# Latent attention: rows of the first two pairs of query tiles loaded ahead, in front of the loads of w_out

## The chip, the cores and the metric

The kernel runs on one core of one Trainium2 chip. The metric is the device time of one execution in microseconds. The engines are TensorE (PE in the rows; PEld is its weight load), VectorE (DVE), ScalarE (ACT), GpSimd (POOL) and SyncE (SP), which here does nothing but issue all transfers between the device memory and the core's buffers.

## What is computed

Two layers. Each one normalises the rows of x (1024 tokens of 1024 numbers), projects them, runs three kinds of heads side by side, projects the joined heads back (w_out) and adds them to x, and then runs a feed-forward block (w_up, w_down). The change is in the second kind of heads, the latent attention, of which this is the reference:

```python
def _mla(cq, ckv, kr, cos, sin, q_norm_g, w_uq, kv_norm_g, w_ukv):
    b, s, _ = cq.shape
    q = (_rmsnorm(cq, q_norm_g) @ w_uq).reshape(b, s, MLA_HEADS, MLA_NOPE + MLA_ROPE)
    qn = q[..., :MLA_NOPE]
    qr = _apply_rope(q[..., MLA_NOPE:], cos[:, :, None, :], sin[:, :, None, :])
    kv = (_rmsnorm(ckv, kv_norm_g) @ w_ukv).reshape(b, s, MLA_HEADS, MLA_NOPE + MLA_V)
    kn, v = kv[..., :MLA_NOPE], kv[..., MLA_NOPE:]
    ...
    def block(args):
        start, qnb, qrb = args
        sc = (jnp.einsum('bqhd,bkhd->bhqk', qnb, kn)
              + jnp.einsum('bqhr,bkr->bhqk', qrb, kr)).astype(jnp.float32) * scale
        p = _masked_softmax(sc, _chunk_mask(start, s))
        return jnp.einsum('bhqk,bkhe->bqhe', p.astype(v.dtype), v)
```

cq has 256 columns and ckv 128, so a tile of 128 tokens has low-rank rows of 128 x 384 numbers. There are 8 such tiles (t = 0 to 7), worked on in four pairs (i = 0 to 3). The mask is causal by chunks of 64 tokens, so pair i needs the keys and values of tiles up to 2i + 1.

## The kernel before

Numbers are 32-bit floats, and each large product is made of three matmuls on numbers split into a high and a low part: L191 to L193 in `mm3`. A split takes ScalarE (L230, the high part) and VectorE (L231, the rest).

**The latent attention.** The in-projection has written the low-rank rows to `d_c` in device memory. `lora(l, st)` loads the weights and gives three functions. `first(t)` loads tile t of `d_c` (L1041, 192 KB), scales it on VectorE (L1042, L1043), and transposes it on TensorE (L1046); `second(t, ...)` multiplies it with w_uq and w_ukv (L1056, L1058); `third` transposes the result (L1085) and splits it (L1089, L1090). In `mla`, `ahead(n, i)` calls them for pair i in four steps, n = 0 to 3. Pair 0 is prepared before the mark `"hidden"`, and pair i + 1 while the scores (L191 to L193, softmax L896 and L897), the product with the values (L922, L909, L938) and the sums of pair i are made.

**What runs beside it.** `mixer` interleaves the instruction streams by `weave`, which always takes the stream that has used the least of a weighted budget. Up to the mark `"hidden"`, the stream of `mla` runs beside the first kind of heads and the end of the in-projection. Then `mla` up to pair 0's heads runs beside the state-space heads (L1230 to L1279, in stream `ip`) and `load_wout`, which loads w_out in 8 pieces of 512 KB (L1288) and splits each on ScalarE (L1292 or L1295) and VectorE (L1296) or GpSimd (L1293). After that, the out-projection (transposes L656, products L191 to L193) runs beside pairs 1 to 3. Before the feed-forward block's first products, each tile of x is normalised (L639), transposed (L212), and its sums and splits are made (L644, L217, L231); its weights w_up come by L270, six narrow loads of 512 KB (128x8x128) first and then wide ones of 1 MB (128x8x256), whose sums are made on GpSimd (L284 to L287) and split. Products are stored to `d_r` by L248. This block is called mlp_up below.

**What sets the order.** All transfers are issued by SyncE, one behind the other: where one waits for its buffer, those behind it wait too. The compiler's scheduler settles each engine's order from the order of the program and from what each instruction waits for. Buffers of one large area (arena_f) are handed out by `Arena`: `get` takes a free place, the one that was given back longest ago, and `put` gives it back. A new holder waits for the old holder's last reader, and so every `get` that is moved or held longer changes the places, and the waits, of later ones, in the whole program.

Of the kernel before, what the change touches and what calls it, by code (L numbers as in the profile page):

```python
# [17 lines left out]
P = 128  # L18
# [12 lines left out]
WOW = 16  # L31
GROUPS = [2] + [4] * 6 + [2, 4]
LEAD = 6
C_Q, C_K, C_V, C_CQ, C_CKV, C_KR, C_Z, C_XBC, C_DT = 0, 256, 512, 768, 1024, 1152, 1184, 1696, 2464

SLOT = 2048
# [70 lines left out]
class Net:  # L107
# [125 lines left out]
    def mlp_up(self, l, hT, bg, late):  # L233
# [27 lines left out]
        N = FF // (2 * P)  # L261
        todo = [(i, True, False) for i in range(LEAD)] + [(i, i >= LEAD, True) for i in range(N)]
        staged = []
# [32 lines left out]
        stage()  # L296
        parts = self.chain(*(forms() for _ in range(LEAD + N)))
        queue = [next(parts) for _ in range(3)]
# [40 lines left out]

        for i in range(LEAD):  # L340
            next(late, None)
# [672 lines left out]
    def lora(self, l, st):  # L1014

        nc, F, I = self.nc, self.F, self.i
        p = st["p"]
        wuq, wukv = F.get(2, 384, top=True), F.get(512, top=True)
# [10 lines left out]
        kr = F.get(8, 32, top=True)  # L1029
# [6 lines left out]
        nc.vector.tensor_add(kr, kr, tmp)  # L1036
        F.put(tmp, k0)

        def first(t):
            cn = F.get(384)  # L1040
            nc.sync.dma_start(cn, self.d_c[l][t * P:t * P + P, 0:384])  # L1041
            nc.vector.tensor_scalar(cn[:, 0:256], cn[:, 0:256], rq[:, t:t + 1], None, op0=ALU.mult)  # L1042
            nc.vector.tensor_scalar(cn[:, 256:384], cn[:, 256:384], rkv[:, t:t + 1], None, op0=ALU.mult)  # L1043
            ps = self.bank("t")[:, 0:384]
            for k in range(3):
                nc.tensor.transpose(ps[:, k * P:k * P + P], cn[:, k * P:k * P + P], self.ident)  # L1046
            F.put(cn)
            cT = F.get(384)
            nc.scalar.copy(cT, ps)
            return cT  # L1050
# [38 lines left out]
                nc.scalar.copy(dst[0:96, :, 0], pv)  # L1089
                nc.vector.tensor_sub(dst[0:96, :, 1], pv, f32(dst[0:96, :, 0]))  # L1090

        return first, second, third, lambda: F.put(kr, wuq, wukv)

    def mla(self, l, st, cc):

        nc, F = self.nc, self.F
        first, second, third, done = self.lora(l, st)
        a, b = {}, {}

        def scores(h, i, pt):  # L1100
            QT, KT = st["QT"][i % 2][:, h], st["KT"][:, h]
            ll, rl = self.sm(2, "ml_l"), self.sm(2, "ml_rl")
            for tt in range(2):
                n = P * (2 * i + tt + 1)
                tok = slice(tt * P, tt * P + P)
                S = self.bank2()
                for c0 in range(0, n, 512):
                    c1 = min(n, c0 + 512)
                    self.mm3(S[:, c0:c1], QT[0:96, 0, tok], QT[0:96, 1, tok],
                             KT[0:96, 0, c0:c1], KT[0:96, 1, c0:c1], True, c1 < n)  # L1110
                nc.tensor.matmul(S[:, n - 64:n], self.chunk[0:96, 0:P], self.chunk[0:96, P:192], start=False, stop=True)  # L1111
                p = F.get(n)
                self.softmax(S, n, p, self.sm(1, "nm"), ll[:, tt:tt + 1])
                pt.append(p)
                yield
            nc.vector.reciprocal(rl, ll)
            pt.append(rl)

        def values(h, i, pt):
            rl = pt.pop()  # L1120
            yield from self.p_times_v(pt[0], pt[1], i, st["vml"][:, :, h], rl, cc[i][:, :, 256 + h * 64:320 + h * 64])
            F.put(*pt)

        def ahead(n, i):
            t = 2 * i
            if n == 0:
                a[t] = first(t)
            elif n == 1:
                a[t + 1] = first(t + 1)
                b[t] = second(t, a.pop(t))  # L1130
            elif n == 2:
                b[t + 1] = second(t + 1, a.pop(t + 1))

        for n in range(3):
            ahead(n, 0)
            yield 2.0
        yield "hidden"
        held, last = iter(()), None
        for i in range(4):
            for t in (2 * i, 2 * i + 1):  # L1140
                third(t, b.pop(t))
                yield 2.0
                next(held, None)
            cc[i] = F.get(2, D, top=True)
            rows = self.d_cc[l][i * 256:i * 256 + 256].rearrange("(t p) e -> p t e", p=P)
            nc.sync.dma_start(cc[i][:, :, 0:256], rows[:, :, 0:256])
            nc.sync.dma_start(cc[i][:, :, 512:1024], rows[:, :, 512:1024])
            for h in range(4):
                pt = []
                for _ in scores(h, i, pt):  # L1150
                    yield 2.0 + 2 * i
                    next(held, None)
                for _ in held:
                    yield 1.0
                if last is not None:
                    yield last
                    last = None
                held = values(h, i, pt)
                if i < 3:
                    ahead(h, i + 1)  # L1160
            last = i
        done()
        for _ in held:
            yield 1.0
        yield last
# [431 lines left out]
```

## Time and profile before

| what | us |
|---|---|
| median of 3 runs | 2828.76 (2823.73 to 2833.22) |
| profiled execution | 2827.39 |
| its span in the trace | 2825.7 |
| TensorE busy in it | 2642.5 (94%) |
| VectorE, ScalarE, GpSimd busy | 1755.9, 1111.0, 587.5 |

TensorE is busy for nearly all of the span, so a gain can come from two things alone: stretches in which TensorE has nothing to do, and stretches in which it runs at the lower of its two clock levels. The mean granted clock of the execution is 0.952 of full speed.

### The profile page before, as it was taken

To read this page: it belongs to the slowest core of one execution; us is meant where nothing else is said; L and a number is where in the kernel's file an instruction comes from. 1 tells how busy PE (TensorE), PEld (TensorE's weight loads), DVE (VectorE), ACT (ScalarE), POOL (GpSimd) and SP (SyncE) were. 2 spreads that over 40 slices of the span, in tenths; PEclk is the share of its full clock that TensorE was granted. 3 is DMA by queue.
4 is the path that set the end of the run, shared out by engine and by line. 5 is a ranking of instruction groups with operands and counts; after the bars stand their busy time and mean duration, and the time that the engine had idled before them with its cause. 6 is when DMAs were issued, how large, how long until landed. Compare 5 with 4: busy or idle time off the path is not lost.

```text
span 2825.7 us, 34756 instructions
## 1 busy us (share of the span) xinstructions
PE 2642.5 (94%) x12530; PEld 2066.1 (73%) x12530; DVE 1755.9 (62%) x3223; ACT 1111.0 (39%) x2145; POOL 587.5 (21%) x517
## 2 busy tenths in 40 slices
PE   5799999899879999999999999988997999999998
PEld 4677776676757777777778777765766888888886
DVE  7767666544867777756585576664459654643435
ACT  5243443544534446121143433354445455621212
POOL 1441233310333220000021113342003522000002
PEclk9899988899989999999999998888998999999999
DMA  6441212322345546534331121132133432541313
GB/s 225 116 137 51 94 50 61 110 73 84 101 150 165 158 148 216 179 122 151 107 119 48 56 91 63 54 101 86 52 105 104 153 116 101 177 149 65 120 47 102
DMA packets 268527, 311.54 MB, mean 110 GB/s; under 512 B 28674, under 2 KB 212164, under 8 KB 268356
## 3 DMA queue, kind: packets, MB, share of 16 engines
q1 hardware_dynamic: 268356, 309.32, 34.0%
q8 instruction: 99, 1.62, 0.2%
q14 instruction: 72, 0.59, 0.1%
HBM read 242.85 MB, written 66.43 MB: 109 GB/s over the span
## 4 chain that ended last, share of the span: by engine, by line
PE 65%; DVE 11%; DMA 7%; issue 2%; ACT 2%; POOL 1%; SPq 0%; DVEq 0%; ACTq 0%; POOLq 0%
PE bank_b L191 9%; PE bank_b L193 9%; PE bank_b L192 9%; PE bank_s L191 8%; PE bank_s L192 8%; PE bank_s L193 8%; PE bank_s L962 3%; DVE split L231 2%; PE bank_a L909 2%; PE bank_t L922 2%; DVE arena_f L570 2%; DMA arena_f<-in_w_ada 1%; DMA d_r<-arena_f 1%; PE bank_s L656 1%; PE bank_a L938 1%
## 5 line engine op out<-in xcount | busy, mean ns | idle before, releaser
L191 PE MATMUL bank_b<-split 128*128 128x512 f32 (+2 forms) x1824 | 728.5, 400 | 51.0 <-ACT split L230 33.1
L192 PE MATMUL bank_b<-split 128*128 128x512 f32 (+2 forms) x1824 | 709.6, 389 | 3.5 <-DVE split L231 3.1
L193 PE MATMUL bank_b<-split 128*128 128x512 f32 (+2 forms) x1824 | 706.5, 389 | 2.9 <-DVE split L231 2.9
L230 ACT CAST split<-arena_f 128x512 fp32r<-128x512 f32 (+1 forms) x424 | 305.8, 747 | 678.3 <-PE bank_s L192 425.8
L191 PE MATMUL bank_s<-split 128*128 128x512 f32 (+2 forms) x1152 | 456.1, 398 | 18.3 <-DVE arena_f L390 6.7
L192 PE MATMUL bank_s<-split 128*128 128x512 f32 (+2 forms) x1152 | 451.2, 392 | 4.4 <-DVE split L231 1.8
L191 PEld LDWEIGHTS bank_b<-split 128*128 128x128 f32 x1824 | 354.1, 194 | 129.5 <-ACT split L230 34.8
L193 PE MATMUL bank_s<-split 128*128 128x512 f32 (+2 forms) x1152 | 448.2, 389 | 0.0
L231 DVE TENSOR_TENSOR split<-arena_f,split 128x512 fp32r<-128x512 f32 (+1 forms) x424 | 381.7, 919 | 92.8 <-ACT split L230 92.0
L193 PEld LDWEIGHTS bank_b<-split 128*128 128x128 f32 x1824 | 352.7, 193 | 71.6 <-DVE split L231 5.0
L192 PEld LDWEIGHTS bank_b<-split 128*128 128x128 f32 x1824 | 354.7, 194 | 68.5 <-issue 4.9
L408 DVE TENSOR_TENSOR arena_f<-arena_f,bank_s 128x1024 f32<-128x1024 f32 x126 | 153.5, 1218 | 230.9 <-PE bank_s L193 230.9
L191 PEld LDWEIGHTS bank_s<-split 128*128 128x128 f32 (+1 forms) x1152 | 218.4, 190 | 73.8 <-DVE arena_f L390 7.4
L192 PEld LDWEIGHTS bank_s<-split 128*128 128x128 f32 (+1 forms) x1152 | 219.5, 191 | 50.4 <-DVE split L231 3.5
L193 PEld LDWEIGHTS bank_s<-split 128*128 128x128 f32 (+1 forms) x1152 | 219.1, 190 | 43.4 <-issue 0.2
L897 ACT ACTIVATE arena_f<-bank_s,nm 128x128 f32<-128x128 f32 (+3 forms) x192 | 141.8, 740 | 191.8 <-DVE nm L896 160.8
L896 DVE TENSOR_REDUCE nm<-bank_s 128x1 f32<-128x128 f32 (+3 forms) x192 | 142.2, 752 | 118.8 <-PE bank_s L1111 64.5
L570 DVE SCALAR_TENSOR_TENSOR arena_f<-arena_f,cond 128x128 f32<-128x128 f32 x448 | 161.7, 387 | 71.4 <-DMA arena_f<-in_b_ada 32.9
L246 ACT ACTIVATE arena_f<-arena_f 128x512 f32<-128x512 f32 x128 | 80.8, 632 | 141.6 <-DVE arena_f L331 69.6
L962 PE MATMUL bank_s<-split 32*128 32x512 f32 (+3 forms) x576 | 124.0, 390 | 12.3 <-ACT arena_f L897 9.1
L925 ACT COPY arena_f<-bank_t 128x512 f32<-128x512 f32 (+1 forms) x160 | 86.8, 542 | 114.1 <-PE bank_t L922 100.9
L696 POOL TENSOR_TENSOR arena_f<-arena_f 128x1024 f32<-128x1024 f32 x14 | 33.6, 2399 | 454.0 <-ACT rstd_y L182 340.0
(281 smaller groups left out, 3207.0 us busy)
## 6 DMA issues: line engine op xcount, KB each, us to landing
arena_f<-in_w_ada SPq DMA_DIRECT2D x80, 512.0 KB
d_r<-arena_f SPq DMA_DIRECT2D x128, 256.0 KB
arena_f<-in_w_up SPq DMA_DIRECT2D x32, 1024.0 KB
arena_f<-in_w_down SPq DMA_DIRECT2D x64, 512.0 KB
arena_f<-d_r SPq DMA_DIRECT2D x64, 512.0 KB
arena_f<-d_x SPq DMA_DIRECT2D x36, 512.0 KB
d_x<-arena_f SPq DMA_DIRECT2D x23, 512.0 KB
arena_f<-in_w_in SPq DMA_DIRECT2D x20, 512.0 KB
```

The source lines that it names most:

```text
L191: mm(out, wh, xh, start=start, stop=False)
L192: mm(out, wh, xl, start=False, stop=False)
L193: mm(out, wl, xh, start=False, stop=stop)
L230: self.nc.scalar.copy(hi, src)
L231: (eng or self.nc.vector).tensor_sub(lo, src, f32(hi))
L246: nc.scalar.activation(t, t, AF.Relu)
L408: nc.vector.tensor_add(y[t], y[t], ps)
L570: nc.vector.scalar_tensor_tensor(acc, in0=w[:, k], scalar=self.cond[:, k:k + 1], in1=acc, op0=ALU.mult, op1=ALU.add)
L896: nc.vector.tensor_reduce(nm, S[:, 0:n], axis=AX.X, op=ALU.max, negate=True)
L897: nc.scalar.activation(p[:, 0:n], S[:, 0:n], AF.Exp, bias=nm, accum_out=ls)
L925: nc.scalar.copy(held, ps[:, 0:w])
L962: nc.tensor.matmul(S[mp][:, c0:c1], Q[rw, a, tok], K[rw, b, c0:c1], start=a == b, stop=a == 1 and c1 < n)
```

## The change

`first(t)` is divided into `load(t)`, which takes the buffer and issues the load, and `first(t, cn)`, which does the rest. `mla` loads tiles 0 and 1 at its start, and tiles 2 and 3 (`EARLY`) when pair 0 is prepared, just ahead of the mark `"hidden"` and so ahead of the loads of w_out in the program. `row(t)` hands out an early buffer or loads the tile as before. In each layer four loads move; no instruction is added or removed, and each early buffer of 384 words is held longer.

```diff
--- before.py
+++ after.py
@@ -31,6 +31,7 @@
 WOW = 16
 GROUPS = [2] + [4] * 6 + [2, 4]
 LEAD = 6
+EARLY = 2, 3
 C_Q, C_K, C_V, C_CQ, C_CKV, C_KR, C_Z, C_XBC, C_DT = 0, 256, 512, 768, 1024, 1152, 1184, 1696, 2464
 
 SLOT = 2048
@@ -1036,9 +1037,12 @@
         nc.vector.tensor_add(kr, kr, tmp)
         F.put(tmp, k0)
 
-        def first(t):
+        def load(t):
             cn = F.get(384)
             nc.sync.dma_start(cn, self.d_c[l][t * P:t * P + P, 0:384])
+            return cn
+
+        def first(t, cn):
             nc.vector.tensor_scalar(cn[:, 0:256], cn[:, 0:256], rq[:, t:t + 1], None, op0=ALU.mult)
             nc.vector.tensor_scalar(cn[:, 256:384], cn[:, 256:384], rkv[:, t:t + 1], None, op0=ALU.mult)
             ps = self.bank("t")[:, 0:384]
@@ -1089,13 +1093,14 @@
                 nc.scalar.copy(dst[0:96, :, 0], pv)
                 nc.vector.tensor_sub(dst[0:96, :, 1], pv, f32(dst[0:96, :, 0]))
 
-        return first, second, third, lambda: F.put(kr, wuq, wukv)
+        return load, first, second, third, lambda: F.put(kr, wuq, wukv)
 
     def mla(self, l, st, cc):
 
         nc, F = self.nc, self.F
-        first, second, third, done = self.lora(l, st)
+        load, first, second, third, done = self.lora(l, st)
         a, b = {}, {}
+        rows = {t: load(t) for t in (0, 1)}
 
         def scores(h, i, pt):
             QT, KT = st["QT"][i % 2][:, h], st["KT"][:, h]
@@ -1121,12 +1126,15 @@
             yield from self.p_times_v(pt[0], pt[1], i, st["vml"][:, :, h], rl, cc[i][:, :, 256 + h * 64:320 + h * 64])
             F.put(*pt)
 
+        def row(t):
+            return rows.pop(t) if t in rows else load(t)
+
         def ahead(n, i):
             t = 2 * i
             if n == 0:
-                a[t] = first(t)
+                a[t] = first(t, row(t))
             elif n == 1:
-                a[t + 1] = first(t + 1)
+                a[t + 1] = first(t + 1, row(t + 1))
                 b[t] = second(t, a.pop(t))
             elif n == 2:
                 b[t + 1] = second(t + 1, a.pop(t + 1))
@@ -1134,6 +1142,8 @@
         for n in range(3):
             ahead(n, 0)
             yield 2.0
+
+        rows.update({t: load(t) for t in EARLY})
         yield "hidden"
         held, last = iter(()), None
         for i in range(4):
@@ -1142,9 +1152,9 @@
                 yield 2.0
                 next(held, None)
             cc[i] = F.get(2, D, top=True)
-            rows = self.d_cc[l][i * 256:i * 256 + 256].rearrange("(t p) e -> p t e", p=P)
-            nc.sync.dma_start(cc[i][:, :, 0:256], rows[:, :, 0:256])
-            nc.sync.dma_start(cc[i][:, :, 512:1024], rows[:, :, 512:1024])
+            src = self.d_cc[l][i * 256:i * 256 + 256].rearrange("(t p) e -> p t e", p=P)
+            nc.sync.dma_start(cc[i][:, :, 0:256], src[:, :, 0:256])
+            nc.sync.dma_start(cc[i][:, :, 512:1024], src[:, :, 512:1024])
             for h in range(4):
                 pt = []
                 for _ in scores(h, i, pt):
```

The scheduler and the arena turn this into other orders on all engines. In what follows, line numbers of the changed kernel are higher: L1042 there is L1041 of before, L1050 is L1046, L1298 is L1288, L1289 is L1279, L1156 and L1157 are L1146 and L1147, L993 is L992; up to L1036 they are higher by one.

SyncE in layer 1, from the load of tile 2 to the next loads of tiles (`d_c`: a tile's rows; `in_w_out`: a piece of w_out; `d_cc`: results of the other heads, stored or loaded). Before:

```order
L1041 DMA arena_f<-d_c_114 128x384
L1279 DMA d_cc_116<-arena_f 128x512
L1288 DMA arena_f<-in_w_out 128x1024 x3
L1147 DMA arena_f<-d_cc_116 128x2x512
L1288 DMA arena_f<-in_w_out 128x1024
L1279 DMA d_cc_116<-arena_f 128x512
L1288 DMA arena_f<-in_w_out 128x1024 x3
L992 DMA d_cc_116<-arena_f 128x8x64
L1146 DMA arena_f<-d_cc_116 128x2x256
L1041 DMA arena_f<-d_c_114 128x384
L1146 DMA arena_f<-d_cc_116 128x2x256
L1147 DMA arena_f<-d_cc_116 128x2x512
```

After the change:

```order
L1289 DMA d_cc_116<-arena_f 128x512
L1042 DMA arena_f<-d_c_114 128x384 x2
L1298 DMA arena_f<-in_w_out 128x1024 x4
L1157 DMA arena_f<-d_cc_116 128x2x512
L1298 DMA arena_f<-in_w_out 128x1024 x3
L1042 DMA arena_f<-d_c_114 128x384
L993 DMA d_cc_116<-arena_f 128x8x64
L1298 DMA arena_f<-in_w_out 128x1024
L1289 DMA d_cc_116<-arena_f 128x512
L1156 DMA arena_f<-d_cc_116 128x2x256
L1042 DMA arena_f<-d_c_114 128x384
L622 DMA arena_f<-d_mod 128x1024
```

Tile 3's load stood behind seven loads of w_out and a store of `d_cc` (L992); now it stands beside tile 2's, ahead of all of them. The last load of w_out stood behind the loads of tiles 3 and 4; now it stands behind tile 4's alone.

TensorE in layer 1, around the transposes of tile 3 (L1046 before, L1050 after; L191 to L193 and L1111 are scores, with L192 to L194 and L1116 after). Before:

```order
L192 MATMUL bank_s<-split 128x128
L193 MATMUL bank_s<-split 128x128
L1111 MATMUL bank_s<-chunk_mask 128x64
L191 MATMUL bank_s<-split 128x256
L192 MATMUL bank_s<-split 128x256
L193 MATMUL bank_s<-split 128x256
L1111 MATMUL bank_s<-chunk_mask 128x64
L1085 MATMUL bank_s<-ident,arena_f 96x128 x8
L1046 MATMUL bank_t<-ident,arena_f 128x128 x3
L922 MATMUL bank_t<-ident,arena_f 128x128 x3
L1056 MATMUL bank_b<-arena_f 128x384 x2
L1058 MATMUL bank_b<-arena_f 128x512
```

After:

```order
L910 MATMUL bank_a<-arena_f 64x256
L910 MATMUL bank_a<-arena_f 64x128
L1050 MATMUL bank_t<-ident,arena_f 128x128 x3
L192 MATMUL bank_s<-split 128x256
L193 MATMUL bank_s<-split 128x256
L194 MATMUL bank_s<-split 128x256
L1116 MATMUL bank_s<-chunk_mask 128x64
L939 MATMUL bank_a<-twice,arena_f 128x64 x2
L923 MATMUL bank_t<-ident,arena_f 128x128 x3
L192 MATMUL bank_s<-split 128x128
L193 MATMUL bank_s<-split 128x128
L194 MATMUL bank_s<-split 128x128
```

The transposes of tile 3 stood behind all scores of pair 0 and behind the eight L1085 of tile 2; now they stand between two groups of scores, ahead of the products L939 and L923.

VectorE in layer 0, at the start of the feed-forward block (L639, L640 after: tile 7 is normalised; L318, L319 after: a product is taken up, the last one from bank_b_6105; L644 and L217, L645 and L218 after: tile 7's transposes are taken up from bank_s_5988; L231, L232 after: splits). Before:

```order
L318 TENSOR_TENSOR arena_f_67<-arena_f_67,bank_b_6069 128x512
L231 TENSOR_TENSOR split_66<-arena_f_67,split_66 128x4x128
L185 TENSOR_SCALAR rstd_t_1_5978<-rstd_y_1_5976,rstd_m_1_5977 128x1
L231 TENSOR_TENSOR split_66<-arena_f_67,split_66 128x512 x2
L186 TENSOR_SCALAR rstd_y_1_5976<-rstd_t_1_5978,rstd_y_1_5976 128x1
L231 TENSOR_TENSOR split_66<-arena_f_67,split_66 128x4x128
L639 SCALAR_TENSOR_TENSOR arena_f_67<-arena_f_67,rstd_y_1_5976 128x1024
L318 TENSOR_TENSOR arena_f_67<-arena_f_67,bank_b_6105 128x512
L644 TENSOR_TENSOR arena_f_67<-bank_s_5988,arena_f_67 128x512
L217 TENSOR_TENSOR arena_f_67<-bank_s_5988,arena_f_67 128x512
L231 TENSOR_TENSOR split_66<-arena_f_67,split_66 128x4x128 x2
```

After, where L640 of tile 7 stands eight rows further up, out of this piece:

```order
L645 TENSOR_TENSOR arena_f_67<-bank_s_5988,arena_f_67 128x512
L218 TENSOR_TENSOR arena_f_67<-bank_s_5988,arena_f_67 128x512
L232 TENSOR_TENSOR split_66<-arena_f_67,split_66 128x4x128
L232 TENSOR_TENSOR split_66<-arena_f_67,split_66 128x512 x2
L232 TENSOR_TENSOR split_66<-arena_f_67,split_66 128x4x128 x2
L319 TENSOR_TENSOR arena_f_67<-arena_f_67,bank_b_6069 128x512
L232 TENSOR_TENSOR split_66<-arena_f_67,split_66 128x4x128
L218 TENSOR_TENSOR arena_f_67<-arena_f_67 128x512 x3
L319 TENSOR_TENSOR arena_f_67<-arena_f_67,bank_b_6105 128x512
L232 TENSOR_TENSOR split_66<-arena_f_67,split_66 128x4x128 x3
L232 TENSOR_TENSOR split_66<-arena_f_67,split_66 128x512 x4
```

Tile 7 was taken up from its transposes behind the last product; now it is taken up ahead of the last two products, and its last splits follow the last product directly.

## Rows read from the trace of the kernel before

**Rows 1.** The page: the span, then from the costliest groups the product matmuls.
```profile
span 2825.7 us, 34756 instructions
...
L191 PE MATMUL bank_b<-split 128*128 128x512 f32 (+2 forms) x1824 | 728.5, 400 | 51.0 <-ACT split L230 33.1
```

**Rows 2.** Waits of TensorE, 1895 to 1925 us (total, times, longest).
```profile
PE bank_t L1046 <- DVE arena_f L1042: 8.7, 1, 8.7
```

**Rows 3.** SyncE, 1840 to 1940 us: start, duration, line, transfer, count.
```profile
1870.84 0.32 SPq L1041 DMA_DIRECT2D arena_f<-d_c  x1
...
1886.12 4.61 SPq L1288 DMA_DIRECT2D arena_f<-in_w_out  x3
...
1898.89 11.01 SPq L1288 DMA_DIRECT2D arena_f<-in_w_out  x3
...
1915.31 0.46 SPq L1041 DMA_DIRECT2D arena_f<-d_c  x1
...
1926.45 0.35 SPq L1288 DMA_DIRECT2D arena_f<-in_w_out  x1
```

**Rows 4.** Chain that ended last, 1880 to 1945 us, in order of time.
```profile
1889.92 3.78 DMA arena_f<-in_w_out
...
1915.31 3.35 DMA arena_f<-d_c
...
1926.45 4.03 DMA arena_f<-in_w_out
...
1937.55 1.77 PE bank_s L656 x8
```

**Rows 5.** Two stretches: width, busy PE, PEld, DVE, ACT, POOL (counts), PEclk, DMA, GB/s.
```profile
1901.70:1925.59 23.89, 11.61 (x36) 7.92 (x36) 13.12 (x42) 8.33 (x20) 10.07 (x8) 0.50 0.39 117
785.80:804.84 19.04, 0.02 (x2) 0.01 (x1) 8.58 (x12) 5.33 (x9) 11.18 (x9) 0.58 0.59 179
```

**Rows 6.** SyncE, 450 to 545 us (layer 0).
```profile
496.07 0.33 SPq L1288 DMA_DIRECT2D arena_f<-in_w_out  x1
...
500.81 0.32 SPq L1041 DMA_DIRECT2D arena_f<-d_c  x1
```

**Rows 7.** Waits of TensorE, 450 to 545 us.
```profile
PE bank_b L1255 <- POOL arena_f L1246: 2.0, 1, 2.0
```

**Rows 8.** ScalarE, 1889 to 1935 us: a split of w_out.
```profile
1930.56 1.15 ACT L1295 ACTIVATE split<-arena_f,cols 128x1024 fp32r<-128x1024 f32 x1 [1.81 <-DMA arena_f<-in_w_out]
```

**Rows 9.** Waits of TensorE, 735 to 812 us (start of mlp_up, layer 0).
```profile
PE bank_b L191 <- ACT split L230: 20.9, 2, 19.0
```

**Rows 10.** Chain that ended last, 765 to 810 us.
```profile
787.08 5.14 DMA d_r<-arena_f
...
792.71 7.79 DMA arena_f<-in_w_up
...
804.16 0.63 ACT split L230
```

**Rows 11.** VectorE, 774 to 812 us: tile 7 and the last product.
```profile
779.50 1.28 DVE L639 SCALAR_TENSOR_TENSOR arena_f<-arena_f,rstd_y 128x1024 f32<-128x1024 f32 x1
785.04 0.69 DVE L318 TENSOR_TENSOR arena_f<-arena_f,bank_b 128x512 f32<-128x512 f32 x1 [4.26 <-PE bank_b L193]
```

**Rows 12.** SyncE, 735 to 800 us: a load of w_up.
```profile
785.85 0.38 SPq L270 DMA_DIRECT2D arena_f<-in_w_up  x1
```

**Rows 13.** GpSimd, 785 to 800 us: first work on that load.
```profile
791.70 1.44 POOL L284 TENSOR_TENSOR arena_f<-arena_f 128x512 f32<-128x512 f32 x1 [16.17 <-DMA arena_f<-in_w_up]
793.22 1.59 POOL L285 TENSOR_TENSOR arena_f<-arena_f 128x512 f32<-128x512 f32 x1
```

**Rows 14.** Waits of TensorE, 2150 to 2195 us (start of mlp_up, layer 1).
```profile
PE bank_b L191 <- ACT split L230: 12.2, 2, 7.6
PE bank_b L192 <- DVE split L231: 3.1, 1, 3.1
```

**Rows 15.** SyncE, 2150 to 2195 us: the last narrow load of w_up.
```profile
2162.15 0.38 SPq L270 DMA_DIRECT2D arena_f<-in_w_up  x1
```

## Prediction

> **What bounds the kernel now.** I read the page first. The profiled execution took 2827.39 us, of which the span is 2825.7 [rows 1]; the other 1.7 lie around it. It is 1.4 us under the median of the three runs, so a sum made against it gets 1.4 added to stand beside that median. TensorE is busy for 94% of the span. The product matmuls of L191 had idle time of 51.0 us in front of them, 33.1 of it ended by the splits of L230 [rows 1]; those splits serve the feed-forward block. So a load that comes earlier is worth only what TensorE waits for it, and the reader should look for the few waits that are long.
>
> Second, TensorE's waits in layer 1's attention. One is long: the transposes of a tile's low-rank rows (L1046) waited 8.7 us for the scaling L1042 [rows 2]. SyncE's rows say why. Tile 2 was loaded at 1870.84, then came w_out from 1886.12; three of its loads, from 1898.89 on, took 11.01 us to get through the queue, and tile 3 was issued at 1915.31 only [rows 3]. The chain of waits agrees: the load took 3.35 us and was on the chain [rows 4]. In layer 0 the same queue did less harm: w_out began at 496.07 and tile 3 was issued at 500.81 [rows 6], and TensorE's list of waits there does not name L1042; the one that hangs on this neighbourhood is L1255's, 2.0 us [rows 7].
>
> Third, the clock in that place. From 1901.70 to 1925.59 the granted clock was 0.50, the lower level (1.2 GHz), and TensorE was busy for 11.61 of 23.89 us [rows 5].
>
> Fourth, the two largest waits outside attention, since a change in buffers reaches them: 19.0 us at the start of mlp_up in layer 0 [rows 9], and 7.6 and 3.1 us at the same place in layer 1 [rows 14].
>
> **Layer 1, attention.** Tile 3's load leaves the place behind seven loads of w_out and the store L992, and stands beside tile 2's; it is issued no later than where w_out began, 1886.12, some 29 us earlier [rows 3]. Its transposes now stand between scores and are covered by them. The wait goes: 8.7 us [rows 2]. The lower clock made 11.61 us of work out of 5.8, so it cost 5.8 us [rows 5]. I count half of it as returned, 2.9: the stretch was idle for 12.3 us, 8.7 by this wait, and the other 3.6 stay and may still bring the clock down. What is late next is the splitting of w_out: ScalarE takes it in order, with the softmax of pair 0 behind it, and there is a row where it waited 1.81 us for a piece to land [rows 8]. I charge one such wait. Sum: -8.7 - 2.9 + 1.8 = -9.8. Bounds: 0 (everything refilled) and -14.5 (both returned in full).
>
> The Trainium skill (page TensorE: Matmul & The Clock Gate, section HAM oscillation) prices the lower clock as half of the whole throttled time. By it this stretch would have cost 11.9 us and the time would come out at 2800. The rows speak against it here: half of the stretch was waiting, which a faster clock does not shorten.
>
> The last load of w_out was issued at 1926.45, took 4.03 us, and the out-projection's transposes came at 1937.55 [rows 4]. It stood behind tiles 3 and 4, and now stands behind tile 4 alone. So the stage's end is no longer held there, and this is why I let the 8.7 us stand as a gain and not as a wait that moves.
>
> **Layer 0, attention.** Tiles 2 and 3 move ahead of w_out's first load, which stood at 496.07. At the worst it goes to where tile 3 was issued, 500.81: +4.7 us [rows 6]. In exchange the scaling no longer stands ahead of the VectorE work that GpSimd's L1246 waits for, on which the 2.0 us of L1255 hang [rows 7]; the order puts it earlier. The loads of w_out have slack here, since their pieces are split beside 20 us of other work. I take -1, between +4.7 and -2.
>
> **The early buffers, and what they shift.** Each of four tiles per layer holds 384 words longer, so `Arena` hands out other places later. At the two places with the longest waits I followed the order by hand.
>
> In mlp_up of layer 0 the wait ended with a split at 804.16. The chain to it: a product is stored for 5.14 us from 787.08, a wide load of w_up in the same place waits for that store and takes 7.79 us from 792.71 [rows 10]. VectorE took up the last product at 785.04; tile 7 was normalised at 779.50, and its transposes and splits followed the product [rows 11]. In the changed order tile 7 is normalised and taken up before the last two products, the first wide load waits for a split right behind the last product, not for the store, and its sums are the first ones needed. Worked out: 785.04 + 0.69 and a split of about the same gives 786.4 for the load. A load of this kind was issued at 785.85 [rows 12] and its first sum began at 791.70 [rows 13], 5.85 us; the two sums end 3.1 us later (793.22 + 1.59), the split takes 0.63: TensorE goes on at 796.0 and not at 804.8. That is -8.8. I take -6, as the loads behind it now share the transfer engines with it. Bounds 0 and -8.8.
>
> In mlp_up of layer 1 tile 7 also moves up, so two wide loads are issued ahead of the last narrow one. The 7.6 and 3.1 us, which waited for sums and for tile 7's splits, then go: -10.7 [rows 14]. But the narrow load, issued at 2162.15 [rows 15], now stands behind 2 MB, of which each wide load took 5.85 us. It lands between 0 and 11.7 us later, and TensorE already waits for it. I take two thirds, 7.7: net -3. Bounds +1 and -10.7.
>
> Everywhere else the orders differ too, by exchanges between neighbours. I found no second wait of such a size, and count 0.
>
> **Sum.** -9.8 - 1 - 6 - 3 = -19.8; 2827.4 - 19.8 = 2807.6, and with the 1.4 of the median 2809.
>
> **Rivals.**
> *Refilled (within 0.3%).* The 8.7 us are taken by the next wait, since SyncE still has to bring 4 MB of w_out in the same stretch, and the places of w_up turn out as bad as before. What speaks for it is that a piece takes 3.78 to 4.03 us to land [rows 4] and that ScalarE already waits for one [rows 8]. Against it stands that w_out now has a clear queue. Only the 2.9 of the clock is left: 2826.
>
> *Attention alone.* The 9.8 us come, mlp_up stays as it was: 2819. For it: the places that I followed hang on one split or store each. Against it: the order of VectorE there has clearly changed.
>
> *More.* All terms reach their lower bounds: -14.5 - 2 - 8.8 - 10.7 = -36, 2793. For it: the same three waits are all long and all moved. Against it: waits of one stage are rarely given back whole.
>
> *Slower.* Splits of w_out hold the softmax. In both layers ScalarE and VectorE take these splits in order between the softmax of pair 0's heads. With eight loads issued in a row, the queue of ScalarE reaches a split before its piece has landed. If it stood a whole landing for each, that is 8 x 3.78 = 30 us in layer 1 alone [rows 4], less the 8.7 and 2.9: +18.6, with the other terms at 0 it ends at 2847. From 1.45 us for each piece on the gain of layer 1 is eaten; from 2.5 us on the kernel is measurably slower. Before, a seen wait is 1.81 [rows 8]. Against it: the loads are issued earlier than before, not later.
>
> *No effect* would be so if the scheduler put tile 3 behind w_out again; the order rules it out in layer 1, and in layer 0 the loads were near each other anyway.
>
> **How the numbers follow.** 0.3% is 8.5 us, about what a measurement of this kernel can tell from no change: faster means under 2820.3, slower above 2837.2. Forecast, between attention alone and somewhat past halfway to the lower bounds (2798 to 2819): 0.46. More: 0.12. Attention alone: 0.12, two thirds of it faster. Refilled: 0.18. Slower: 0.12. That makes 0.66 faster, 0.22 the same, 0.12 slower. The range goes from the lower bounds, 2793, to where the unpriced terms are at their upper ends with the attention's gain gone, 2828.8 + 4.7 + 1 = 2834; what lies outside is mostly the slower rival.
>
> **What would show it.** Tile 3's load in layer 1 issued ahead of w_out, L1046 without a wait over 2 us there, and the granted clock over 0.5 for most of the next 20 us: the first term is right. The last load of w_out some 10 us earlier against tile 4's: the end of the stage is free. In mlp_up of layer 0, one wait of about 10 us in place of 19.0; in layer 1, a longer wait ahead of the last narrow load's product and none behind it. The prediction is wrong if TensorE waits there for L897 behind splits of w_out, or if a new wait of over 5 us stands at a place where before had none, since then the places handed out anew cost what I counted as nothing.

## The result

The changed kernel took 2800.43 us (median of 4 runs, 2799.98 to 2802.63), the kernel before 2826.24 (4 runs, 2820.72 to 2833.22) beside it: ratio 0.9909, 95% interval 0.9882 to 0.9935. That is faster by 25.8 us, 18 to 33 by the interval. Run a second time, beside 18 other runs of the kernel before, it came out at 0.9936 (0.9911 to 0.9960). All ratios here and below leave out two executions in a slow state, one of the kernel before (7854.11 us) and one of spare, an experiment below (2998.24 us).

The page of the changed kernel gives the span, TensorE's busy time and the product matmuls (L192 is L191 of before, as all line numbers below are higher):

```profile
span 2798.3 us, 34743 instructions
...
PE 2636.9 (94%) x12530; PEld 2059.5 (74%) x12530; DVE 1748.4 (62%) x3223; ACT 1110.0 (40%) x2145; POOL 581.9 (21%) x517
...
L192 PE MATMUL bank_b<-split 128*128 128x512 f32 (+2 forms) x1824 | 725.1, 398 | 37.5 <-ACT split L231 22.2
```

Span less busy time is TensorE's idle time. It was 2825.7 - 2642.5 = 183.2 us and is 161.4 now, 21.8 less; the busy time fell by 5.6. Idle time before the products of this group fell from 51.0 to 37.5 us [rows 1]. So four fifths of this profile's gain of 27.4 us are waiting that is gone. Where it went is seen by cutting both executions at the same products (the orders differ, so a piece can hold a few matmuls more or less): attention of layer 0, the start of mlp_up there, attention of layer 1, mlp_up there, and the first part of mlp_down of layer 1. Windows of before (width, then the busy time of PE, PEld, DVE, ACT and POOL, the granted clock, the transfer engines' share, GB/s):

```profile
349.20:715.10 365.90, 343.08 (x1746) 251.06 (x1745) 211.52 (x485) 166.97 (x372) 86.59 (x79) 0.90 0.25 80
753.00:837.80 84.80, 61.90 (x259) 49.08 (x257) 60.10 (x96) 36.33 (x64) 37.94 (x26) 0.84 0.38 122
1532.10:1975.20 443.10, 417.85 (x2131) 315.13 (x2129) 264.53 (x574) 187.77 (x448) 123.83 (x106) 0.92 0.23 72
2119.30:2243.80 124.50, 107.18 (x460) 86.61 (x461) 98.80 (x150) 63.63 (x114) 53.42 (x34) 0.92 0.39 129
2352.60:2529.60 177.00, 177.00 (x782) 146.41 (x781) 85.06 (x108) 84.65 (x123) 18.49 (x14) 1.00 0.40 136
```

The same five pieces after the change:

```profile
350.30:700.60 350.30, 328.26 (x1754) 241.14 (x1752) 207.88 (x485) 167.52 (x373) 88.07 (x78) 0.95 0.26 84
734.80:816.00 81.20, 63.02 (x258) 49.36 (x257) 61.45 (x87) 38.73 (x69) 36.21 (x27) 0.89 0.38 123
1507.30:1946.80 439.50, 422.41 (x2131) 318.70 (x2130) 267.23 (x574) 187.83 (x449) 117.63 (x106) 0.91 0.24 74
2091.00:2208.50 117.50, 105.97 (x467) 86.04 (x466) 95.61 (x154) 64.41 (x117) 49.98 (x32) 0.96 0.42 137
2317.30:2502.60 185.30, 179.76 (x781) 147.93 (x781) 86.77 (x108) 84.93 (x123) 19.30 (x14) 0.98 0.39 130
```

Width less PE is the idle time of a piece. It goes from 22.8 to 22.0, from 22.9 to 18.2, from 25.2 to 17.1, from 17.3 to 11.5, and in the last piece from nothing to 5.5: a gain of 13.9 net, and 7.9 lie scattered over the rest. The first piece is 15.6 us shorter, but by TensorE's busy time (14.8 less) and the clock (0.90 to 0.95), not by waits. The experiments show that this part belongs to the run and not to the kernel.

**Attention of layer 1.** SyncE's rows, answering to [rows 3], show tiles 2 and 3 issued together, ahead of all w_out:

```profile
1867.14 1.24 SPq L1042 DMA_DIRECT2D arena_f<-d_c  x2
1871.27 7.99 SPq L1298 DMA_DIRECT2D arena_f<-in_w_out  x4
...
1881.11 5.93 SPq L1298 DMA_DIRECT2D arena_f<-in_w_out  x3
1890.96 0.33 SPq L1042 DMA_DIRECT2D arena_f<-d_c  x1
...
1894.54 0.53 SPq L1298 DMA_DIRECT2D arena_f<-in_w_out  x1
```

TensorE's longest waits from 1860 to 1905 us, answering to [rows 2], are

```profile
PE bank_s L193 <- DVE split L1094: 1.8, 1, 1.8
PE bank_t L923 <- ACT arena_f L898: 1.2, 2, 0.6
```

and the wait of 8.7 us is gone. In this profile the low clock is not; the stretch that answers to [rows 5] is

```profile
1883.60:1900.70 17.10, 16.12 (x51) 10.48 (x50) 15.48 (x42) 10.42 (x28) 8.51 (x8) 0.50 0.58 193
```

**Start of mlp_up.** TensorE's waits in layer 0, 735 to 812 us, answering to [rows 9], and below them GpSimd's first work on the wide load [rows 13]:

```profile
PE bank_b L192 <- ACT split L231: 14.1, 2, 10.4
```

```profile
780.12 1.26 POOL L285 TENSOR_TENSOR arena_f<-arena_f 128x512 f32<-128x512 f32 x1 [4.17 <-DMA arena_f<-in_w_up]
781.46 1.26 POOL L286 TENSOR_TENSOR arena_f<-arena_f 128x512 f32<-128x512 f32 x1
```

The 19.0 us have become 10.4. The load now waits for a split behind the last product, as was read from the order, and its sums are the first that are needed. The chain of waits, 755 to 790 us, shows it, answering to [rows 10]:

```profile
773.19 0.69 DVE arena_f L319
773.88 1.22 DVE split L232 x2
775.11 7.63 DMA arena_f<-in_w_up
782.76 0.63 ACT split L231
```

In layer 1 the waits [rows 14] have become (2091 to 2209 us)

```profile
PE bank_b L192 <- ACT split L231: 6.7, 2, 6.2
PE bank_s L213 <- DVE arena_f L640: 3.6, 1, 3.6
```

**A new wait, in mlp_down of layer 1.** Before, TensorE had none there. Now two waits, 3.9 and 1.6 us, 5.5 in all, stand before L192, for the copy L407. The chain of waits tells their cause, in order of time:

```profile
2434.21 1.23 DVE split L232
...
2435.46 7.84 DMA arena_f<-d_r
...
2443.32 1.05 ACT split L231
2444.37 0.92 ACT arena_f L407
```

A load of `d_r` gets its place only when a split has read it out, takes 7.84 us, and the split that waits for it on ScalarE stands ahead of the copy that would free TensorE's bank.

### The profile page after: what moved, and what is told of

Same layout as the page of the kernel before. It is cut to its first block, busy times and chain, and to the rows that moved or that the text cites. A ratio compares the mean times of both kernels' runs of the same rounds, so it can differ in the third digit from the quotient of the medians.

```text
span 2798.3 us, 34743 instructions
## 1 busy us (share of the span) xinstructions
PE 2636.9 (94%) x12530; PEld 2059.5 (74%) x12530; DVE 1748.4 (62%) x3223; ACT 1110.0 (40%) x2145; POOL 581.9 (21%) x517
## 4 chain that ended last, share of the span: by engine, by line
PE 67%; DVE 11%; DMA 5%; ACT 3%; issue 2%; POOL 1%; SPq 0%; DVEq 0%; ACTq 0%; POOLq 0%
PE bank_b L192 10%; PE bank_b L194 10%; PE bank_b L193 10%; PE bank_s L192 8%; PE bank_s L193 8%; PE bank_s L194 8%; PE bank_a L910 3%; DVE split L232 2%; PE bank_s L963 2%; PE bank_t L923 2%; DVE arena_f L571 1%; PE bank_b L1265 1%; PE bank_s L657 1%; PE bank_b L1060 1%; PE bank_a L939 1%
## 5 line engine op out<-in xcount | busy, mean ns | idle before, releaser
L192 PE MATMUL bank_b<-split 128*128 128x512 f32 (+2 forms) x1824 | 725.1, 398 | 37.5 <-ACT split L231 22.2
L193 PE MATMUL bank_b<-split 128*128 128x512 f32 (+2 forms) x1824 | 706.2, 387 | 1.7 <-DVE split L232 1.3
L194 PE MATMUL bank_b<-split 128*128 128x512 f32 (+2 forms) x1824 | 706.3, 388 | 1.4 <-DVE split L232 1.4
L231 ACT CAST split<-arena_f 128x512 fp32r<-128x512 f32 (+1 forms) x424 | 304.4, 748 | 661.2 <-PE bank_s L193 427.4
L192 PE MATMUL bank_s<-split 128*128 128x512 f32 (+2 forms) x1152 | 457.0, 399 | 20.8 <-DVE arena_f L391 6.9
L193 PE MATMUL bank_s<-split 128*128 128x512 f32 (+2 forms) x1152 | 451.9, 392 | 5.2 <-DVE split L1094 1.8
L232 DVE TENSOR_TENSOR split<-arena_f,split 128x512 fp32r<-128x512 f32 (+1 forms) x424 | 385.6, 928 | 107.6 <-ACT split L231 107.0
L194 PE MATMUL bank_s<-split 128*128 128x512 f32 (+2 forms) x1152 | 449.1, 390 | 0.0
L192 PEld LDWEIGHTS bank_b<-split 128*128 128x128 f32 x1824 | 351.9, 193 | 117.3 <-ACT split L231 24.6
L194 PEld LDWEIGHTS bank_b<-split 128*128 128x128 f32 x1824 | 350.5, 192 | 70.7 <-DVE split L232 3.7
L193 PEld LDWEIGHTS bank_b<-split 128*128 128x128 f32 x1824 | 351.6, 193 | 67.9 <-issue 5.5
L192 PEld LDWEIGHTS bank_s<-split 128*128 128x128 f32 (+1 forms) x1152 | 218.9, 190 | 77.5 <-ACT arena_f L407 7.7
L193 PEld LDWEIGHTS bank_s<-split 128*128 128x128 f32 (+1 forms) x1152 | 219.8, 191 | 51.8 <-DVE split L232 3.5
L194 PEld LDWEIGHTS bank_s<-split 128*128 128x128 f32 (+1 forms) x1152 | 219.7, 191 | 44.7 <-issue 1.1
L898 ACT ACTIVATE arena_f<-bank_s,nm 128x384 f32<-128x384 f32 (+4 forms) x192 | 142.1, 742 | 180.0 <-DVE nm L897 149.0
L963 PE MATMUL bank_s<-split 32*128 32x512 f32 (+3 forms) x576 | 115.9, 382 | 11.3 <-ACT arena_f L898 8.1
```

The lines of the kernel that those rows point to most:

```text
L192: mm(out, wh, xh, start=start, stop=False)
L193: mm(out, wh, xl, start=False, stop=False)
L194: mm(out, wl, xh, start=False, stop=stop)
L231: self.nc.scalar.copy(hi, src)
L232: (eng or self.nc.vector).tensor_sub(lo, src, f32(hi))
L898: nc.scalar.activation(p[:, 0:n], S[:, 0:n], AF.Exp, bias=nm, accum_out=ls)
```

## The experiments

All on one core, each beside runs of the kernel before on the same chip. "Idle" is the span less TensorE's busy time, both from the page of the profiled execution; the rows of before and of the first run of the change stand on top.

| kernel | ratio to before (95%) | span | PE busy | idle |
|---|---|---|---|---|
| before | 1 | 2825.7 | 2642.5 | 183.2 |
| the change | 0.9909 (0.9882 to 0.9935) | 2798.3 | 2636.9 | 161.4 |
| before_again | 2833.13 us, a single run | 2831.4 | 2643.8 | 187.6 |
| shift | 1.0044 (1.0019 to 1.0069) | 2838.1 | 2657.9 | 180.2 |
| same_places | 1.0007 (0.9989 to 1.0025) | 2816.0 | 2627.6 | 188.4 |
| spare | 1.0013 (0.9994 to 1.0033) | 2825.4 | 2631.4 | 194.0 |
| late_load | 0.9919 (0.9895 to 0.9943) | 2796.1 | 2633.4 | 162.7 |
| held_back | 0.9924 (0.9900 to 0.9948) | 2818.3 | 2649.2 | 169.1 |
| l1_only | 0.9955 (0.9929 to 0.9981) | 2808.6 | 2631.1 | 177.5 |
| two_three | 0.9891 (0.9866 to 0.9915) | 2787.9 | 2622.3 | 165.6 |
| after_again | 0.9936 (0.9911 to 0.9960) | 2795.9 | 2630.6 | 165.3 |
| two_three_again | 0.9911 (0.9885 to 0.9936) | 2794.8 | 2624.5 | 170.3 |
| three | 0.9923 (0.9890 to 0.9957) | 2816.2 | 2645.2 | 171.0 |
| two_to_four | 0.9950 (0.9933 to 0.9967) | 2803.4 | 2642.9 | 160.5 |

Two theories stood against each other. By the first, the queue: tile 3's load no longer stands behind w_out, and the 8.7 us go for that. By the second, the places: buffers taken early shift which place each later `get` finds, and with it what each load waits for, in the whole program.

**The kernel before, run again (before_again), and moved in time (shift).** In the first nothing is edited; the second only lengthens the start:

```diff
-        nc.vector.tensor_mul(self.cond, c8, e8)
+        for _ in range(24):
+            nc.vector.tensor_mul(self.cond, c8, e8)
```

Expected of before_again: 

> The kernel before, profiled once more, for its stretches at the lower clock. In its first profile two stretches of 20.5 us at the lower clock (from 358.9 and 430.6 us) lie where TensorE had no gap and where TensorE's order is the same as after the change; after the change they are absent, and some 16 us of the 27 us gained come from there. Theory A (they belong to this program's timing): they come again within a few us of the same places, and layer 0 from 349 to 715 us again loses about 35 us to the clock. Theory B (they fall by chance in any run): they are at other places or absent, and the run is up to 20 us shorter.

Expected of shift: 

> The kernel before with one multiplication of the start-up (128 x 8, on VectorE) done 24 times in place of once, so that all that follows runs some 2 to 3 us later in the same order. Theory 'clock by chance of phase': the stretches at the lower clock in layer 0 move or go, and the time changes by 10 us or more in either direction. Otherwise: before plus 0 to 4 us, with the two stretches of 20.5 us in place.

In layer 0, before and before_again have two stretches at the lower clock in which TensorE is busy all the time. Windows of before, and behind them of shift:

```profile
358.90:379.40 20.50, 20.50 (x65) 15.23 (x62) 15.17 (x37) 7.01 (x16) 7.53 (x6) 0.50 0.19 64
430.60:451.10 20.50, 20.50 (x63) 15.04 (x62) 18.34 (x58) 6.77 (x16) 5.77 (x5) 0.50 0.14 36
```

```profile
363.80:384.30 20.50, 20.50 (x65) 15.03 (x64) 15.31 (x37) 7.01 (x16) 7.69 (x6) 0.50 0.18 61
435.50:456.00 20.50, 20.50 (x62) 14.94 (x62) 18.68 (x60) 6.78 (x16) 5.78 (x5) 0.50 0.12 31
```

They moved with the program, by 4.9 us. The change's first profile has none of it: from 349.2 to 446.6 us the granted clock is 1.00. That explains its shorter attention in layer 0. But they come back in held_back, which has the change's early buffers, and they are missing in same_places, which has the order of before on all engines up to about 491 us, and in l1_only, whose layer 0 is that of before. So they belong to the execution, not to the change. What sets them off was not found.

The runs of shift came out at 1.0044 of before, 12.5 us more where 0 to 4 were expected. Some 5 of them are the longer start itself, by which all that follows moved. In its profile the idle time (180.2) is not longer than before's, and TensorE's busy time is 15.4 us longer (2657.9), at mean granted clocks of 0.945 to 0.954 over its runs; so the rest goes with the clock.

**The early loads with all other places as before (same_places).** Tiles 2 and 3 are loaded ahead into places that were picked by hand; every other `get` is handed the place that it had before, from a written list. Tiles 0 and 1 aren't moved.

```diff
-            cn = F.get(384)
+            cn = F.get(384, at=AT.get((l, t)))
...
-        at = self._find(m, top)
+        at = next(self.places) if at is None else at
```

Expected: 

> Tiles 2 and 3 are loaded early as in the change, tiles 0 and 1 are not moved, and every other buffer has the place it had before (the places are written out as a list), so that waits for buffers elsewhere stay as before. Theory 'queue' (the gain is the load that no longer stands behind w_out): layer 1's wait of 8.7 us goes, 19.0 us in mlp_up of layer 0 and 7.6 and 3.1 in layer 1 stay; 2814 to 2820. Theory 'places' (most of it is the buffers handed out anew): within 4 us of before, 2822 to 2830. Theory 'clock' (most of it is layer 0's clock, which any other order loses or not): anything from 2800 to 2826, with the difference in layer 0 ahead of 470 us.

Ratio 1.0007: nothing. But this didn't settle it as meant, since SyncE did not issue tile 3 any earlier in layer 1:

```profile
1874.84 4.61 SPq L1359 DMA_DIRECT2D arena_f<-in_w_out  x3
1885.23 0.33 SPq L1359 DMA_DIRECT2D arena_f<-in_w_out  x1
1887.44 10.64 SPq L1359 DMA_DIRECT2D arena_f<-in_w_out  x3
1903.02 0.33 SPq L1103 DMA_DIRECT2D arena_f<-d_c  x1
```

That its place is given back late, and the scheduler puts a load where its buffer is free and not where the code writes it, is the likely reason; late_load bears on it. The wait before its transposes stayed, at 7.3 us. In layer 0, however, tile 2's load did move ahead of w_out (475.05, and w_out from 484.86), with the places of before, and the wait at mlp_up there was 19.1: loading early did not shorten that one.

**The buffers early, the loads written at the old place (late_load).**

```diff
         def load(t):
-            cn = F.get(384)
-            nc.sync.dma_start(cn, self.d_c[l][t * P:t * P + P, 0:384])
-            return cn
+            return F.get(384)
 
         def first(t, cn):
+            nc.sync.dma_start(cn, self.d_c[l][t * P:t * P + P, 0:384])
```

Expected: 

> The buffers are taken when the change takes them, so that all places are those of the change, but each load is issued where it was before, inside first(t). Theory 'queue': layer 1's wait for the scaling of tile 3 comes back (8 to 9 us), mlp_up keeps its gain; 2805 to 2812 against 2800 of the change. Theory 'places': as the change, 2798 to 2803. Theory 'clock': not foretold by the waits; if layer 0 from 349 to 715 us loses 35 us to the clock again, 2815 to 2825.

Ratio 0.9919, as the change. SyncE's order is that of the change, with the two loads at 1866.26, ahead of w_out. The line on which a load stands does nothing here; the buffer decides. So this run does not part the two theories either.

**Tile 3 behind w_out again, all places as in the change (held_back).** In layer 1, one column of tile 3's buffer is first overwritten from the newest split of w_out, so that its load can't be issued earlier.

```diff
-            nc.sync.dma_start(cn, self.d_c[l][t * P:t * P + P, 0:384])
+            if (l, t) != (1, 3):
+                nc.sync.dma_start(cn, self.d_c[l][t * P:t * P + P, 0:384])
...
-            return rows.pop(t) if t in rows else load(t)
+            if (l, t) != (1, 3):
+                return rows.pop(t) if t in rows else load(t)
+            cn = rows.pop(t)
+            nc.vector.tensor_copy(cn[:, 0:1], f32(st["wo"][-1][:, 1, 0:1]))
+            nc.sync.dma_start(cn, self.d_c[l][t * P:t * P + P, 0:384])
+            return cn
```

Expected: 

> The change, but tile 3's load in layer 1 waits, by one added copy of a single column on VectorE, until the newest split piece of w_out is there; the order then puts it behind seven loads of w_out again, while all buffers keep the places of the change. Theory 'queue': TensorE's wait for the scaling of tile 3 is back (7 to 10 us) and the time is 7 to 10 us over the change: ratio to before 0.994 to 0.996. Theory 'places' (the queue is worth nothing, another wait stands there anyway): as the change, 0.990 to 0.993.

```profile
1888.56 7.99 SPq L1304 DMA_DIRECT2D arena_f<-in_w_out  x4
1898.39 6.04 SPq L1304 DMA_DIRECT2D arena_f<-in_w_out  x3
1905.67 0.33 SPq L1135 DMA_DIRECT2D arena_f<-d_c  x1
```

Tile 3 stands behind seven loads of w_out, as before the change, and the ratio is 0.9924. TensorE's longest waits in this place, 1880 to 1920 us:

```profile
PE bank_s L192 <- ACT arena_f L898: 4.4, 2, 3.8
PE bank_s L193 <- DVE split L1095: 1.8, 1, 1.8
```

Its layer-1 attention is idle for 22.0 us (441.50 wide, 419.53 busy) against 17.1 in the change and 25.2 before, in one profile each. So the position in the queue is worth some 5 us of idle time in this stage, too little for the ratios to tell. The rest of the gain comes without it. But only the position is that of before: the load is issued 17.1 us behind the first of w_out (1888.56, 1905.67), where before it was 29.2 (1886.12, 1915.31), as the loads of w_out get through faster here. What the full delay would cost in the order of the change was not measured.

**Buffers held, loads as before (spare).** Empty buffers of 384 words are held as long as the change holds its early ones; the loads take their own, late.

```diff
+        spare = {t: F.get(384) for t in (0, 1)}
...
+        spare.update({t: F.get(384) for t in (2, 3)})
```

Expected: 

> The kernel before, with empty buffers of 384 words taken where the change takes its early ones and given back when the tile has been transposed; each load still has a buffer of its own, taken as before. So the places of all later buffers shift as by the change, and nothing is loaded early by intent. Theory 'queue': as before, 0.998 to 1.002. Theory 'places': a shift of places is worth some 10 to 20 us by itself, of either sign: 0.990 to 0.996 or 1.004 to 1.010, with the waits at the start of mlp_up changed.

Ratio 1.0013. The places shift here too, and nothing is gained: 18.4 us at mlp_up of layer 0, and in layer 1's attention a wait of 9.8 us at another line:

```profile
PE bank_t L922 <- ACT arena_f L1049: 9.8, 1, 9.8
```

So a shift of places isn't a gain as such. It counts which shift.

**Layer 1 alone (l1_only).**

```diff
-        rows = {t: load(t) for t in (0, 1)}
+        rows = {t: load(t) for t in (0, 1) if l == 1}
...
-        rows.update({t: load(t) for t in EARLY})
+        rows.update({t: load(t) for t in EARLY if l == 1})
```

Expected: 

> The change in layer 1 alone; layer 0 is as before. From the idle time by stage of the changed kernel (layer 1: attention -8.2, start of mlp_up -5.8, later products +5.5 us) theory 'queue and places, each where it stands' gives about -8 us: ratio 0.996 to 0.998, with layer 0's 19.0 us wait unchanged. Theory 'all in layer 0' gives 0.999 to 1.001, theory 'all in layer 1' 0.990 to 0.993.

Ratio 0.9955, about half of the first gain (0.9909) and two thirds of the second (0.9936). The wait at mlp_up of layer 0 stays as it was, so its shortening is the doing of layer 0's early buffers:

```profile
PE bank_b L192 <- ACT split L231: 21.3, 2, 19.0
```

The new wait in mlp_down of layer 1 is not there: this piece has no idle time, as before. Layer 0 alone was not run.

**Which tiles (two_three, two_three_again, three, two_to_four, and after_again beside them).** In all but after_again, tiles 0 and 1 are loaded as before, and `EARLY` names the tiles ahead.

```diff
-        rows = {t: load(t) for t in (0, 1)}
+        rows = {}
```

Expected of two_three: 

> The change for tiles 2 and 3 alone; tiles 0 and 1 are loaded inside first(t) as before. Theory 'queue': tiles 0 and 1 never stood behind w_out, so as the change, 0.990 to 0.993. Theory 'places': the places fall out otherwise again, and the waits in mlp_up (19.0 and 7.6 us before) change by more than 3 us against the change.

Expected of after_again: 

> The change, run again with more rounds beside the three that follow. Expected 0.991 of before, 0.9885 to 0.9935. In its profile the same waits of TensorE as in the first: 10.35 us at the start of mlp_up in layer 0, 6.25 us at the same place in layer 1, and a new one of 3.9 us before L192 in mlp_down of layer 1, since the order of the instructions is the same. If lower-clock stretches of 20.5 us at about 359 and 431 us stand in this profile, which were absent in the first one of the change, they belong to the run and not to the kernel; then its layer-0 attention is about 18 us longer than in the first profile.

Expected of two_three_again: 

> Tiles 2 and 3 loaded ahead, tiles 0 and 1 as in the kernel before. Theory: the early loads of tiles 0 and 1 give nothing, so this is as fast as the change or up to 6 us faster: ratio to before 0.9875 to 0.992, and below that of the change in the same job by 0 to 0.003. Rival: 0.9891 was a matter of the clock in that run, and it comes out above the change, at 0.992 to 0.995.

Expected of three: 

> Tile 3 alone loaded ahead, tiles 0, 1 and 2 as in the kernel before. If the queue position of tile 3's load made the gain, this has it too: 0.989 to 0.993. If the places made it, then each set of early buffers deals them anew and this comes out anywhere between 0.988 and 1.001, with the waits at the two starts of mlp_up (19.0 us, and 7.7 and 3.1 us before) changed in one direction or the other; what TensorE is idle there in the profile should then account for the difference to the run of tiles 2 and 3.

Expected of two_to_four: 

> Tiles 2, 3 and 4 loaded ahead, tiles 0 and 1 as before. Tile 4's load then leaves the place ahead of the last load of w_out too. By the queue theory a further 1 to 4 us: 0.988 to 0.990. By the places theory anywhere between 0.988 and 1.001, again with the difference standing as idle time of TensorE at the starts of mlp_up and in mlp_down.

No gain from tiles 0 and 1 is seen: without them 0.9891 and 0.9911, with them 0.9909 and 0.9936, beside the same runs of before 0.0025 apart with intervals that overlap. Tiles 2 and 3 alone are the best version measured, not shown to be faster than the change. Their waits differ from the change's, by other places. In mlp_up of layer 0:

```profile
PE bank_b L192 <- ACT split L231: 6.1, 1, 6.1
PE bank_s L213 <- DVE arena_f L640: 3.6, 1, 3.6
PE bank_b L192 <- DVE arena_f L319: 3.3, 1, 3.3
```

and in layer 1

```profile
PE bank_b L192 <- ACT split L231: 14.5, 1, 14.5
```

where the change has 6.2. Tile 3 alone has 10.0 and 5.5 us as the longest waits at these two places. Tile 4 with them gives the least idle time of all, 160.5, and a smaller gain, 0.9950, where the queue theory asked for 0.988 to 0.990; TensorE's busy time of 2642.9 takes it back, and the mean granted clock of its runs has the median 0.956, with 0.9585 in after_again. Whether that order brings the clock down or its runs happened to, stays open.

## Why the prediction was right, and where not

The forecast was 2809, a ratio of 2809 / 2828.8 = 0.9930; the order of the change measured 0.9909, 0.9919 (late_load) and 0.9936. Idle time of 16.9 us was predicted to go (the sum of 19.8 less the 2.9 of the clock), and 21.8 went in the first profile, 17.9 in after_again (both against the first profile of before).

- **Layer 1's attention, the wait (-8.7, +1.8).** Right in size: the wait is gone, and the stage is idle for 8.2 us less. The charge of 1.8 did not come due: ScalarE's waits for pieces of w_out were 6.4 us in all before (1880 to 1945 us, six of them) and are 2.3 now (1866 to 1935 us, one of 1.8 and one of 0.5), and no wait in TensorE's list names these splits. So *Slower* fell. Less right in its cause: with tile 3 back behind w_out (held_back) the wait of 8.7 did not come back, but one of 3.8, and the stage was still idle for 3.2 us less than before. That this rest hangs on the order that the places made was not tested by itself.
- **Layer 1's attention, the clock (-2.9).** This step failed. Half of what the low clock cost in the stretch of [rows 5] was to come back with the wait. With the wait gone, the clock was in the first profile again 0.50 for 17.10 us, now with TensorE busy for 16.12 of them: work that cost 8.1 us more than at the full clock, where before it was 5.8. Over the stage the granted clock went from 0.92 to 0.91, and busy time rose by 4.6, so that the stage is only 3.6 us shorter. A second profile of each shows how far this scatters: in after_again the clock was low for 3.4 us from 1880.9 (TensorE busy for 3.40) and 6.8 us from 1891.2 (busy for 5.85), a cost of 4.6; in before_again for 20.5 us from 1907.3 (busy for 9.01), a cost of 4.5. So the stretch itself was shorter after the change in both, but what it costs was not: 8.1 and 4.6 against 5.8 and 4.5.
- **The Trainium skill's price of the clock.** The Trainium skill's rule (page TensorE: Matmul & The Clock Gate, section HAM oscillation) would have given 2800, and the time is 2800.4. The agreement says nothing for it: in the first profile the stretch that it priced came again, and the work in it cost 8.1 us.
- **The end of the stage.** The last w_out load was expected some 10 us earlier against tile 4's. It moved the other way: before, it was issued 0.6 us behind tile 4's (1925.84, 1926.45), now 3.6 us (1890.96, 1894.54). It cost nothing that can be seen: from 1895 to 1950 us TensorE has no wait over 0.4 us.
- **Layer 0's attention (-1).** Idle time fell by 0.8.
- **mlp_up of layer 0 (-6).** Right, by the mechanism that was followed in the order: 10.4 us instead of 19.0, 4.7 less idle in the stage (18.2 for 22.9), as other short waits took some of it. l1_only shows that it is layer 0's early buffers, and same_places that tile 2's load ahead of w_out, without their places, does not do it.
- **mlp_up of layer 1 (-3).** Mis-sized: -5.8. The 7.6 and 3.1 us went. The wait for the narrow load was to grow by 7.7 (two thirds of 11.7 would be 7.8); it went from 4.6 [rows 14] to 6.2 only. The wait for tile 7's normalisation (L639, L640 after), which the sum left out, went from 1.2 to 3.6.
- **"Everywhere else 0".** Wrong in a term: mlp_down of layer 1 is 8.3 us longer, 5.5 of it idle. The prediction named a new wait of over 5 us as what would make it wrong; the two waits here reach that together, the longer alone is 3.9. It was paid for by waits scattered elsewhere, 7.9 us less in the first profile. In after_again the total gain in idle time is 17.9, so this scatter is no fixed gain. That the total came out so near was luck in this part: neither the loss in mlp_down nor the scatter that covers it was foreseen, nor that the charge of 1.8 would fall away and the 2.9 of the clock with it.

*Refilled* is out by the ratio. *Attention alone* is out too: mlp_up did change in both layers. *More* asked for 36 us.

## What to carry to other kernels

When buffers come from a pool, loading earlier is two edits: the transfer moves, and every later buffer is dealt anew; here most of the gain stayed when the load was held back with its buffer in place, and part of it was paid out some 270 us later (mlp_up of layer 0) and further on. Read from the order where the new buffers make the longest waits of the profile begin, and test the two apart by holding the load back. Compare the idle time of the engine that bounds the kernel beside the times, where runs of one kernel lay up to 32 us apart with the clock: it was 180 to 194 us in the profiles of the kernels that gained nothing and 160 to 178 in those that gained. Within these groups it tells little: two profiles of one kernel differ by up to 4.7 us, and the least idle time (two_to_four) went with one of the smaller gains.

## What the runs showed of the hardware

- The lower clock comes over TensorE while it is busy, too: two stretches of 20.5 us, busy for all of it, at granted clock 0.50. They stood in the profiles of before, before_again, shift and held_back, and in none of the change, after_again, late_load, same_places, spare, l1_only, two_to_four and both of two_three; three has one, of 17.1 us. The work done in the two costs 20.5 us more than at the full clock (an estimate: 41.0 us of busy time at half of it), nearly as much as the whole change gives.
- Runs of one kernel follow the mean clock: the 18 runs of before that stand beside after_again go from 2814.76 us at 0.957 to 2846.93 at 0.946.
